# One raster for two operand pools, four changes of order, and later scales in a hybrid decoder trunk on one core

## The chip, the cores and the metric

The kernel runs on one core of one Trainium2 chip. The metric is the device time of one execution in microseconds (us). Engines: PE (TensorE; its weight loads are listed as PEld), DVE (VectorE), ACT (ScalarE), POOL (GpSimd), and SP (SyncE), which issues almost all DMAs in program order.

## The reference, cut to what matters

The kernel computes a two-layer trunk for 1,024 tokens and 1,024 channels in fp32.

```python
h = x
for layer in range(2):
    hn = rmsnorm(h, g_mix[layer])
    # layer 0: [b | c | x | u | v] = hn @ w_in ; gated conv (b, c, x) and spatial gating (u, v)
    # layer 1: latent attention (8 heads, causal) and a chunked matrix memory (4 heads)
    h = h + concat(branch_a, branch_b) @ w_out
    h = h + (silu(n @ w_gate) * (n @ w_up)) @ w_down          # n = rmsnorm(h, g_ffn), inner width 2816
    h = h + sigmoid(rmsnorm(h, g_ple) @ w_ple_gate) * (p[layer] @ w_ple_proj)
```

## The kernel before

**Split products.** Each fp32 operand is split into a high part (a cast to float32r, on ACT) and a low part (the remainder, on DVE): `split`, lines 146 and 147. A product of two split operands is three matmuls, in `mm3`: high x high at L189, high x low at L190, low x high at L191 (names in the trace end in h and l, or begin with them). Almost all of PE's work is such matmuls with 512 columns. The weights come in as fp32 tiles with the tag `raw` and are split into tiles `whi` and `wlo`.

**Memory.** Each pool is a range of SBUF addresses, the same in every partition. Pools lie one behind the other in the order in which they are opened: `const`, `opB` (operand slots 0 to 31, and others), `w` (`raw`, `whi`, `wlo`), `tmp` (temporaries, some of a few bytes), and behind them `opA` (slots 32 and up, `B.cp`), which is closed and opened again between stages, with the attention's pools in the same place. Operand tiles are 2,048 bytes per partition in all of them. From the sizes of the tiles: `opB` and `whi`/`wlo` tiles start at 832 modulo 2,048, and `opA` tiles at 1,984, since the small tiles of `tmp` lie between.

**Which operand lies where.** Both token halves of a matrix (n = 0 and 1) go through most products. In `opA` lie: all of x0 (the transposed input, `x_group`), 24 of the 40 slot numbers that `xc` takes (`free` at L452: 32 to 53, 54, 55; 16 to 31 are in `opB`), the half n = 1 of xp, and wj and pT of the output gates. In `opB` or `w` lie: xb, mix, act, xn, the half n = 0 of xp, and all other weights.

**Stages** (us of the profiled execution): input projection zv with token-major output 15 to 73; spatial gating (pu, pm) 73 to 132; conv branches (pc, px, pb) 132 to 266; output projection (po); FFN up and gate products (p) ; FFN down (pd) 690 to 988; gates and embedding (ppg, ppj) to 1,085; layer 1's projections to 1,378; attention with the memory interleaved to 1,600; the same tail again, with pd to 2,325 and `ple_out` from there to the end.

**Order.** A scheduler moves instructions within each engine, but the order in the code decides most. `later(d, fn)` calls fn after d more groups of matmuls (`tick`). `x_scale` makes the token scales of one half of the input: eight squares on ACT (L904, names junk and xt), then a reciprocal root, then `bcast_prep`, which puts the high and low parts of the scales on two diagonals dg, one on DVE and one on POOL; `bcast` multiplies both by ones on PE (Rb, L298 and L299), and ACT copies the sum to R. `norm_later` does the same elsewhere. In the gating, ug = pu * R on DVE (L1037) frees the PSUM bank of pu, then pm follows. `v_done` is the chain behind each tile of zv: gv on ACT, its square gvs on POOL, a reduction, a root, a product and a split on DVE. At the last keys, `heads_out` transposes k on PE (kTt), splits it on ACT and DVE, and stores it to kT_d; `load_head` reads K and Q of a head back (two tiles of 96 x 1,024 each). `mq_part(g, n)` is 24 matmuls for the memory's queries. `ple_out` transposes p (`make_pT`: ptr on PE, then a split into pTh and pTl), and per tile of 128 tokens multiplies gates (ppg) and embedding (ppj).

Of the kernel before, what the change touches and what calls it, by code (L numbers as in the profile page):

```python
# [11 lines left out]
F32 = mybir.dt.float32  # L12
# [9 lines left out]
P = 128  # L22
# [24 lines left out]
class Build:  # L47
# [60 lines left out]
    def w_part(self, srcs, kt, cols, name, gcol, slots=None):  # L108
        nc = self.nc
        raw = self.wp.tile([P, kt, cols], F32, tag="raw", name=self.name(f"r{name}"), bufs=RAW)  # L110
        o = 0
# [43 lines left out]
    def w_quarter(self, w, rows, c, name):  # L155

        t = self.wp.tile([P, 4, P], F32, tag="raw", name=self.name(f"r{name}"), bufs=RAW)
        self.nc.sync.dma_start(
            t, w[rows * HT : (rows + 1) * HT, c].rearrange("(k p) c -> p k c", p=P)
        )  # L160
        return t
# [7 lines left out]
    def w_chain(self, w, c0, c1, name, eng):  # L169


        tt = eng.tensor_tensor
        raw = lambda: self.wp.tile([P, 4, P], F32, tag="raw", name=self.name(f"s{name}"), bufs=RAW)
        a11 = self.w_quarter(w, 0, c0, name)
        a21 = self.w_quarter(w, 0, c1, name)
        a22 = self.w_quarter(w, 1, c1, name)
        a12 = self.w_quarter(w, 1, c0, name)
        s1, s2 = raw(), raw()
        tt(out=s1, in0=a21, in1=a22, op=ALU.add)
        tt(out=s2, in0=s1, in1=a11, op=ALU.subtract)  # L180
        tt(out=a21, in0=a11, in1=a21, op=ALU.subtract)
        return {1: a11, 2: a12, 4: a22, 5: s1, 6: s2, 7: a21}
# [95 lines left out]
    def bcast_prep(self, r):  # L278
# [6 lines left out]
        out = []  # L285
        for i, x in enumerate((rh.bitcast(F32), rl)):
            d = self.tmp("dg", (P, 4, P), F32R)
            (nc.vector, nc.gpsimd)[i].tensor_tensor(
                out=d, in0=self.ident.unsqueeze(1).to_broadcast([P, 4, P]),
                in1=x.unsqueeze(2).to_broadcast([P, 4, P]), op=ALU.mult,  # L290
            )
            out.append(d.rearrange("p a b -> p (a b)"))
# [32 lines left out]
def trunk(ctx, tc, x, p, positions, g_mix, g_ffn, g_ple, ev_w_in, ev_w_conv, ev_g_v, ev_w_s,  # L325
# [10 lines left out]
    B.wp = ctx.enter_context(tc.tile_pool(name="w", bufs=1))  # L336
    B.tp = ctx.enter_context(tc.tile_pool(name="tmp", bufs=1))

# [318 lines left out]
    def ffn_down(l, act_d, h_d, h2_d, X2, st, normed):  # L657
# [7 lines left out]
        def part(fh, ch, f, t=None):  # L665
            if t is None:
                t = B.wp.tile([P, HT], F32, tag="raw", name=B.name("rd"), bufs=RAW)
            r = (fh * half + f) * P
# [165 lines left out]
    def ple_out(l, tok, h2_d, X, r):  # L834

        pT = {}
        for n in range(2):
            pT[n] = make_pT(load_p(l, n) if n else tok, [32 + 4 * n + i for i in range(4)])
        for cg in range(2):
# [8 lines left out]
            for k in range(2):  # L848
                raw = B.wp.tile([P, HT], F32, tag="raw", name=B.name("rpj"), bufs=RAW)
                nc.sync.dma_start(raw, w_ple_proj[l][k * P : (k + 1) * P, c])  # L850
                a = B.slots2(40 + 4 * cg + 2 * k, 41 + 4 * cg + 2 * k, "wj")
                B.split(a[0], a[1], raw)
                wj.append(a)
            for tt in range(NT):
                n, t = tt // 4, slice((tt % 4) * P, (tt % 4 + 1) * P)
                pg = B.tm_mm(grp, X, tt, "ppg")
                pj = B.ps("ppj")
# [41 lines left out]
    def x_scale(n):  # L899
# [16 lines left out]

        B.later(2, fn)

    pv = B.ps_tr("pvec", (P, 16))
    nc.tensor.transpose(pv, rows0, ident[0:16, 0:16])  # L920
    nc.vector.tensor_copy(vec[:, 0:16], pv)
    for q in range(2):
        for kk in range(4):
            x_group(0, q, kk)
    zv_unit = B.w_unit(w_in[0:512, 2048:2560], 4, HT, "zva", G_MIX)
# [58 lines left out]
    for tt in range(NT):  # L984
        ps = B.tm_mm((zv_unit, HT), X, tt, "zv")
        if tt == 1:
# [3 lines left out]
        if tt < 4:  # L990
            for kk in range(2):
                x_group(1, tt // 2, (tt % 2) * 2 + kk)
            if tt == 3:
                x_scale(1)
        elif tt < 6:
            ws_T(tt - 4)
        elif tt == 6:
            u0 = u_unit(0, ((28, 29), (30, 31)))
# [84 lines left out]
    def rest(l, XC, second_half, h_d, out, rtok=None, full=True):  # L1083
# [4 lines left out]
        X2, st = newX(), {}  # L1088
        normed = lambda n: B.norm_later(st, n, 2 - n, out, rtok, full)
        prepare, run = ffn_down(l, act_d, h_d, h2_d, X2, st, normed)  # L1090
# [151 lines left out]
    def up_weights(src, kt, cols, gcol, name):  # L1242
        pairs = []
        half = cols // 2
        for k in range(kt):
# [3 lines left out]
            for i in range(2):  # L1249
                c = slice(i * half, (i + 1) * half)  # L1250
                raw = B.wp.tile([P, half], F32, tag="raw", name=B.name(f"r{name}"), bufs=RAW)
                nc.sync.dma_start(raw, src[k * P : (k + 1) * P, c])
# [282 lines left out]
    for n in range(2):  # L1535
        t = mq_part(0, n, B.ps("mq"))
        if kprev:
            heads_out(*kprev.pop(), ksc, kT_d, "kT")
# [15 lines left out]
    def load_head(h):  # L1554
        t = []
        for nm, src in (("K", kT_d), ("Q", qT_d)):
            for i in range(2):
                a = tp.tile([QK, T], F32R, tag=f"{nm}{i}", name=B.name(f"{nm}{i}"), bufs=2)
                nc.sync.dma_start(a.bitcast(F32), src[i][:, h, :].bitcast(F32))
                t.append(a)  # L1560
        return t

# [287 lines left out]
    for i, u in enumerate(units):  # L1850
# [5 lines left out]
        if i == 0:  # L1856
            mq_part(1, 0, psum("O", "mq", 1))
            att_scores(u)
            att_exp(u)
            ahead = 1  # L1860
            mq_part(1, 1, psum("m", "mq", 1))
            mem = mem_all()
# [82 lines left out]
```

## Time and profile before

| | us |
|---|---|
| median of 3 runs (lowest to highest) | 2453.76 (2452.49 to 2454.29) |
| profiled execution: its time | 2453.51 |
| profiled execution: span in the trace | 2451.8 |
| outside the span | 1.7 |
| PE busy | 2413.6 |
| DVE, ACT, POOL busy | 1561.2, 988.2, 679.8 |
| mean granted clock of PE | 0.999 |

Busy time of a matmul runs from its start to its modelled end; neighbours overlap, so that a 512-column matmul shows 389 ns where the next one starts some 227 ns behind it. PE is busy for nearly the whole span: a gain has to shorten matmuls or close the gaps that are left.

### The profile page before, as it was taken

To read this page: it belongs to the slowest core of one execution; us is meant where nothing else is said; L and a number is where in the kernel's file an instruction comes from. 1 tells how busy PE (TensorE), PEld (TensorE's weight loads), DVE (VectorE), ACT (ScalarE), POOL (GpSimd) and SP (SyncE) were. 2 spreads that over 40 slices of the span, in tenths; PEclk is the share of its full clock that TensorE was granted. 3 is DMA by queue.
4 is the path that set the end of the run, shared out by engine and by line. 5 is a ranking of instruction groups with operands and counts; after the bars stand their busy time and mean duration, and the time that the engine had idled before them with its cause. 6 is when DMAs were issued, how large, how long until landed. Compare 5 with 4: busy or idle time off the path is not lost.

```text
span 2451.8 us, 33875 instructions
## 1 busy us (share of the span) xinstructions
PE 2413.6 (98%) x11510; PEld 1993.8 (81%) x11510; DVE 1561.2 (64%) x3079; ACT 988.2 (40%) x1877; POOL 679.8 (28%) x678
## 2 busy tenths in 40 slices
PE   7999999999999999999999999999999999999999
PEld 6878887788888888888888788878788888888877
DVE  6864479645556778776785566548855455687731
ACT  5322244233233545444554455635333232454520
POOL 3452121546553000112321132111256556100000
PEclk9999999999999999999999999999999999999999
DMA  4221453433236966553454843154433233886721
GB/s 151 78 86 48 136 169 101 141 99 112 91 108 204 308 226 214 174 173 96 114 154 121 228 112 106 46 168 134 129 120 112 87 111 103 286 281 210 251 97 39
DMA packets 358685, 350.74 MB, mean 143 GB/s; under 512 B 24011, under 2 KB 249648, under 8 KB 358512
## 3 DMA queue, kind: packets, MB, share of 16 engines
q1 hardware_dynamic: 358016, 348.25, 45.3%
q8 instruction: 90, 1.47, 0.2%
q0 software_dynamic: 464, 0.33, 0.1%
q14 instruction: 83, 0.68, 0.1%
q10 hardware_dynamic: 32, 0.01, 0.0%
HBM read 255.18 MB, written 93.32 MB: 142 GB/s over the span
## 4 chain that ended last, share of the span: by engine, by line
PE 52%; DVE 4%; issue 2%; DMA 1%; ACT 1%; POOL 0%; SPq 0%; DVEq 0%; POOLq 0%; ACTq 0%
PE p L190 5%; PE p L189 5%; PE p L191 5%; PE pd L189 3%; PE pd L190 3%; PE pd L191 3%; PE O L1833 2%; PE ppg L191 2%; PE ppg L190 2%; PE ppg L189 2%; PE PT L1875 1%; PE po L189 1%; PE po L190 1%; PE po L191 1%; PE S L1775 1%
## 5 line engine op out<-in xcount | busy, mean ns | idle before, releaser
L189 PE MATMUL pd<-acth,hd 128*128 128x512 f32 x616 | 240.0, 390 | 0.1
L190 PE MATMUL pd<-actl,hd 128*128 128x512 f32 x616 | 239.7, 389 | 0.0
L191 PE MATMUL pd<-acth,ld 128*128 128x512 f32 x616 | 239.7, 389 | 0.0
L189 PE MATMUL p<-xch,hg 128*128 128x512 f32 x440 | 173.1, 394 | 5.3 <-DVE sg L534 2.2
L190 PE MATMUL p<-xcl,hg 128*128 128x512 f32 x440 | 173.1, 393 | 0.2
L189 PE MATMUL p<-xch,hu 128*128 128x512 f32 x440 | 173.0, 393 | 0.0
L191 PE MATMUL p<-xch,lu 128*128 128x512 f32 x440 | 172.9, 393 | 0.0
L191 PE MATMUL p<-xch,lg 128*128 128x512 f32 x440 | 172.9, 393 | 0.0
L190 PE MATMUL p<-xcl,hu 128*128 128x512 f32 x440 | 172.6, 392 | 0.0
L541 POOL TENSOR_TENSOR act<-act,sg 128x512 f32<-128x512 f32 x60 | 90.0, 1499 | 244.1 <-DVE act L534 239.3
L146 ACT CAST hu<-ru 128x512 fp32r<-128x512 f32 x116 | 71.6, 622 | 183.3 <-PE p L190 170.4
L189 PEld LDWEIGHTS pd<-acth,hd 128*128 128x128 f32 x616 | 115.6, 188 | 24.3 <-DVE res L728 0.5
L191 PEld LDWEIGHTS pd<-acth,ld 128*128 128x128 f32 x616 | 115.6, 188 | 24.3
L146 ACT CAST hg<-rg 128x512 fp32r<-128x512 f32 x110 | 68.2, 620 | 165.9 <-PE p L190 135.6
L190 PEld LDWEIGHTS pd<-actl,hd 128*128 128x128 f32 x616 | 115.6, 188 | 23.8
L147 DVE TENSOR_TENSOR lu<-ru,hu 128x512 fp32r<-128x512 f32 x116 | 117.2, 1011 | 14.9 <-ACT hu L146 14.9
L146 ACT CAST hd<-rd 128x512 fp32r<-128x512 f32 x110 | 68.3, 621 | 133.5 <-PE pd L190 82.2
L147 DVE TENSOR_TENSOR actl<-ra,acth 128x512 fp32r<-128x512 f32 x154 | 109.5, 712 | 12.1 <-ACT acth L146 12.0
L259 POOL TENSOR_TENSOR S<-S,sq 128x512 f32<-128x512 f32 x38 | 51.6, 1359 | 219.7 <-ACT sq L257 219.7
L147 DVE TENSOR_TENSOR ld<-rd,hd 128x512 fp32r<-128x512 f32 x110 | 76.9, 699 | 47.6 <-ACT hd L146 47.6
L189 PEld LDWEIGHTS p<-xch,hg 128*128 128x128 f32 x440 | 82.6, 188 | 26.5 <-ACT hg L146 3.0
L146 ACT CAST acth<-ra 128x512 fp32r<-128x512 f32 x154 | 94.7, 616 | 13.1 <-DMA ra<-act 9.3
(561 smaller groups left out, 6615.9 us busy)
## 6 DMA issues: line engine op xcount, KB each, us to landing
ra<-act SPq DMA_DIRECT2D x154, 256.0 KB, 3.7
rd<-in_w_down SPq DMA_DIRECT2D x154, 256.0 KB, 4.0
rg<-in_w_gate SPq DMA_DIRECT2D x100, 256.0 KB, 3.3
ru<-in_w_up SPq DMA_DIRECT2D x100, 256.0 KB, 2.9
act<-act SPq DMA_DIRECT2D x88, 256.0 KB, 2.0
act<-at SPq DMA_DIRECT2D x66, 256.0 KB, 2.0
rpg<-in_w_ple_gate SPq DMA_DIRECT2D x48, 256.0 KB, 3.0
sd<-in_w_down SPq DMA_DIRECT2D x44, 256.0 KB, 4.2
```

The source lines that it names most:

```text
L146: self.nc.scalar.copy(hi, src)
L147: (eng or self.nc.vector).tensor_tensor(out=lo, in0=src, in1=hi.bitcast(F32), op=ALU.subtract)
L189: mm(ps, a[0], b[0], start=first, stop=False, skip_group_check=more)
L190: mm(ps, a[0], b[1], start=False, stop=False, skip_group_check=more)
L191: mm(ps, a[1], b[0], start=False, stop=last, skip_group_check=more)
L259: eng.tensor_tensor(out=st[n], in0=st[n], in1=sq, op=ALU.add)
L541: (nc.vector if last else nc.gpsimd).tensor_tensor(out=t, in0=t, in1=sg[d["i"], key], op=ALU.mult)
L1775: mm(s[:, 0:w], q0, K0[:, c0 : c0 + w], start=True, stop=False)
L1833: nc.tensor.matmul(O[h][:, b * DV : (b + 1) * DV], t[:, j * P : (j + 1) * P], V[h // 2][:, kb, (h % 2) * DV : (h % 2 + 1) * DV], start=kb ...
L1875: nc.tensor.transpose(pt[:, j * P : (j + 1) * P], e[:, j * P : (j + 1) * P], ident)
```

## The change

Five edits. (1) `raw` moves to a pool of its own, and it and `tmp` go to the right end of SBUF (side="right"), so that `opA` and the attention's pools come right behind `w`. Worked out from the tile sizes, `opA` tiles then start at 832 modulo 2,048, as `opB` and `whi`/`wlo` do; `raw` goes from 832 to 2,016 and `tmp` from 832 to 864. (2) At the start, the first tile of zv runs its k-tiles 0 to 3 before the transposes for 4 to 7; the second half's transposes come four behind tile 1 and four behind tile 2 instead of two behind each of 0 to 3; `ws_T` and `u0` come one tile later, Rb two groups later. (3) In `bcast_prep` both diagonals are made on DVE. (4) The scales at the end of FFN down come at 2 + 2n groups instead of 2 - n. (5) The last `heads_out` follows `mq_part(0, 1)` instead of `mq_part(0, 0)`; head 0 is loaded in pieces; both `mq_part(1, n)` come before the first scores; and in `ple_out` the gate products of a tile are issued one tile ahead of its embedding product.

```diff
@@ w_part, and the same in four other places
-        raw = self.wp.tile([P, kt, cols], F32, tag="raw", name=self.name(f"r{name}"), bufs=RAW)
+        raw = self.rp.tile([P, kt, cols], F32, tag="raw", name=self.name(f"r{name}"), bufs=RAW)
@@ bcast_prep
-        for i, x in enumerate((rh.bitcast(F32), rl)):
+        for x in (rh.bitcast(F32), rl):
             d = self.tmp("dg", (P, 4, P), F32R)
-            (nc.vector, nc.gpsimd)[i].tensor_tensor(
+            nc.vector.tensor_tensor(
@@ trunk
     B.wp = ctx.enter_context(tc.tile_pool(name="w", bufs=1))
-    B.tp = ctx.enter_context(tc.tile_pool(name="tmp", bufs=1))
+    B.rp = ctx.enter_context(tc.tile_pool(name="raw", bufs=1, side="right"))
+    B.tp = ctx.enter_context(tc.tile_pool(name="tmp", bufs=1, side="right"))
@@ ple_out
-        for n in range(2):
-            pT[n] = make_pT(load_p(l, n) if n else tok, [32 + 4 * n + i for i in range(4)])
+        p_slots = lambda n: [32 + 4 * n + i for i in range(4)]
...
+            pgs = [B.tm_mm(grp, X, 0, "ppg")]
+            if cg == 0:
+                pT[0] = make_pT(tok, p_slots(0))
+                tok = load_p(l, 1)
             for tt in range(NT):
                 n, t = tt // 4, slice((tt % 4) * P, (tt % 4 + 1) * P)
-                pg = B.tm_mm(grp, X, tt, "ppg")
+                if tt + 1 < NT:
+                    pgs.append(B.tm_mm(grp, X, tt + 1, "ppg"))
+                if cg == 0 and tt == 1:
+                    pT[1] = make_pT(tok, p_slots(1))
+                pg = pgs[tt]
@@ x_scale
-        B.later(2, fn)
+        B.later(4, fn)
@@ input projection
-    for q in range(2):
-        for kk in range(4):
-            x_group(0, q, kk)
+    for kk in range(4):
+        x_group(0, 0, kk)
...
-        ps = B.tm_mm((zv_unit, HT), X, tt, "zv")
+        if tt == 0:
+            ps = B.ps("zv")
+            for k in range(KT):
+                if k == 4:
+                    for kk in range(4):
+                        x_group(0, 1, kk)
+                a = X[0][k]
+                B.mm3(ps, (a[0][:, 0:P], a[1][:, 0:P]), zv_unit[k], k == 0, k == KT - 1)
+            B.tick()
+        else:
+            ps = B.tm_mm((zv_unit, HT), X, tt, "zv")
...
-            for kk in range(2):
-                x_group(1, tt // 2, (tt % 2) * 2 + kk)
+            if tt in (1, 2):
+                for kk in range(4):
+                    x_group(1, tt - 1, kk)
@@ rest
-        normed = lambda n: B.norm_later(st, n, 2 - n, out, rtok, full)
+        normed = lambda n: B.norm_later(st, n, 2 + 2 * n, out, rtok, full)
@@ last keys
         t = mq_part(0, n, B.ps("mq"))
-        if kprev:
+        if n == 1:
             heads_out(*kprev.pop(), ksc, kT_d, "kT")
@@ load_head
+        if h == 0:
+            last, rest = slice(T - P, T), slice(0, T - P)
+            for nm, i, c in (("Q", 0, last), ("K", 0, slice(0, T)), ("Q", 1, last),
+                             ("K", 1, slice(0, T)), ("Q", 0, rest), ("Q", 1, rest)):
+                part(nm, i, c)
@@ attention, first unit
-            mq_part(1, 0, psum("O", "mq", 1))
+            for n in range(2):
+                mq_part(1, n, psum(("O", "m")[n], "mq", 1))
             att_scores(u)
             att_exp(u)
             ahead = 1
-            mq_part(1, 1, psum("m", "mq", 1))
```

Three places in the order of issue. First, ACT in the input projection, before the change, around the last two casts of the second half's x0 (x0h_571 and x0h_580); the junk rows are the last two of eight squares over the second half, vh belongs to `v_done`:

```order
L904 ACTIVATE junk_597,ss_584<-xt_264 128x512
L904 ACTIVATE junk_599,ss_584<-xt_266 128x512
L146 CAST vh_151_537<-gv_146_516 128x512
L146 CAST x0h_571<-xT_566 128x512
L146 CAST x0h_580<-xT_575 128x512
L934 ACTIVATE gv_177_626<-zv_541,rt_287 128x512
```

The same place with the change; the last two casts are x0h_519 and x0h_528, and junk_588 is the first of the eight squares:

```order
L146 CAST x0h_501<-xT_496 128x512
L146 CAST x0h_510<-xT_505 128x512
L146 CAST vh_135_467<-gv_130_446 128x512
L146 CAST x0h_519<-xT_514 128x512
L146 CAST x0h_528<-xT_523 128x512
L912 ACTIVATE junk_588,ss_587<-xt_219 128x512
```

The eight squares stood ahead of the last two casts and now stand behind them. Second, PE at the first scores, before (S is a tile of scores, mq_13298 is `mq_part(1, 1)`; 12 of its matmuls stand behind the first score, and the last here is the first of them):

```order
L190 MATMUL mq_13298<-xnl_2361_9896,hmq_0_2953_13086 128x512
L191 MATMUL mq_13298<-xnh_2360_9895,lmq_0_2954_13087 128x512
L1775 MATMUL S_13279<-K_2967_13182,Q_2969_13186 128x512
L1776 MATMUL S_13279<-K_2968_13184,Q_2969_13186 128x512
L1775 MATMUL S_13283<-K_2967_13182,Q_2969_13186 128x512
L1776 MATMUL S_13283<-K_2968_13184,Q_2969_13186 128x512
L189 MATMUL mq_13298<-xnh_2376_9960,hmq_4_2956_13092 128x512
```

The same place with the change (mq_13284 is `mq_part(1, 1)`; S_13348 belongs to the second unit of scores):

```order
L190 MATMUL mq_13284<-xnl_2413_10107,hmq_4_2956_13095 128x512
L191 MATMUL mq_13284<-xnh_2412_10106,lmq_4_2957_13096 128x512
L1807 MATMUL S_13313<-K_2968_13187,Q_2967_13185 128x512
L1808 MATMUL S_13313<-K_2970_13191,Q_2967_13185 128x512
...
L1809 MATMUL S_13317<-K_2968_13187,Q_2969_13189 128x512
L1811 LDWEIGHTS identb
L1811 MATMUL S_13317<-maskq,identb 128x128
L1807 MATMUL S_13348<-K_2968_13187,Q_2967_13185 128x512
```

All of mq now stands ahead of the first score, and no mq between the first unit of scores and the second. Third, PE in `ple_out` of layer 1, before, where the first ppj stands; ppg_22835 is the first tile of gates:

```order
L189 MATMUL ppg_22835<-hpg_7_5443_22803,xph_22543 128x512
L189 MATMUL ppj_22880<-wjh_22825,pTh_22724 128x512
L190 MATMUL ppj_22880<-wjl_22826,pTh_22724 128x512
L189 MATMUL ppg_22897<-hpg_0_5422_22761,xph_22116 128x512
L190 MATMUL ppg_22897<-lpg_0_5423_22762,xph_22116 128x512
L792 MATMUL ptr_22741<-ident,ptok_22737 128x128 x2
L191 MATMUL ppj_22880<-wjh_22825,pTl_22725 128x512
```

With the change, where the transposes ptr and the first ppj stand; ppg_22800 and ppg_22847 are the first and the second tile of gates:

```order
L191 MATMUL ppg_22800<-hpg_7_5429_22768,xpl_22549 128x512
L793 MATMUL ptr_22825<-ident,ptok_22642 128x128 x2
...
L189 MATMUL ppg_22847<-hpg_0_5408_22726,xph_22121 128x512
...
L191 MATMUL ppg_22847<-hpg_7_5429_22768,xpl_22549 128x512
L189 MATMUL ppj_22872<-wjh_22790,pTh_22830 128x512
L190 MATMUL ppj_22872<-wjl_22791,pTh_22830 128x512
```

A whole tile of gates (24 matmuls) now stands between the transposes and the first ppj, and the transposes for the second half no longer stand in the middle of the first ppj.

## Rows read from the trace of the kernel before

**Rows 1.** Page, part 1: busy time, share of the span, instructions.

```profile
PE 2413.6 (98%) x11510; PEld 1993.8 (81%) x11510; DVE 1561.2 (64%) x3079; ACT 988.2 (40%) x1877; POOL 679.8 (28%) x678
```

**Rows 2.** Groups of PE by form: line, tile, count; busy, mean ns; idle before.

```profile
L190 PE MATMUL pd<-actl,hd 128*128 128x512 f32 x616 | 239.7, 389 | 0.0
...
L190 PE MATMUL p<-xcl,hg 128*128 128x512 f32 x440 | 173.1, 393 | 0.2
...
L191 PE MATMUL p<-xbh,lg 128*128 128x512 f32 x176 | 68.6, 390 | 0.0
...
L190 PE MATMUL pc<-x0l,hc 128*128 128x512 f32 x64 | 25.3, 395 | 0.0
```

**Rows 3.** Tile ppg on PE, 985 to 1030 us: ns min/median/max, starts.

```profile
L190 PE MATMUL ppg<-xpl,hpg x33: 389/389/395, 1000.1 to 1029.8; 128*128 128x512 f32 x33
```

**Rows 4.** The same, 1040 to 1085 us.

```profile
L190 PE MATMUL ppg<-xpl,hpg x50: 389/392/404, 1040.1 to 1084.6; 128*128 128x512 f32 x50
```

**Rows 5.** Windows, PE alone: window, length, PE busy, clock, DMA share, GB/s.

```profile
800.00:920.00 120.00, 120.00 (x531) 1.00 0.80 265
```

**Rows 6.** Waits of PE over the span: us in total, times, longest.

```profile
PE zv L189 <- ACT x0h L146: 4.0, 1, 4.0
...
PE S L1775 <- DMA Q<-qTd: 1.7, 1, 1.7
PE pm L189 <- DVE ug L1037: 1.7, 1, 1.7
...
PE kTt L1290 <- DVE k L1503: 1.5, 1, 1.5
...
PE ptr L792 <- DVE lpg L147: 1.0, 1, 1.0
...
PE ppj L189 <- ACT pTh L146: 0.7, 1, 0.7
```

**Rows 7.** Timeline of ACT: start us, us, instruction.

```profile
46.25 0.64 ACT L904 ACTIVATE junk<-xt 128x512 f32<-128x512 f32 x1
...
51.67 1.06 ACT L146 CAST x0h<-xT 128x512 fp32r<-128x512 f32 x2
```

**Rows 8.** Windows: length; busy of PE, PEld, DVE, ACT, POOL; clock; DMA.

```profile
48.00:56.00 8.00, 3.99 (x14) 2.65 (x13) 7.22 (x25) 5.36 (x17) 0.89 (x1) 0.79 0.14 38
...
70.00:90.00 20.00, 20.00 (x88) 16.11 (x87) 18.81 (x42) 6.79 (x12) 10.14 (x10) 1.00 0.38 107
90.00:110.00 20.00, 20.00 (x105) 16.94 (x104) 17.25 (x32) 6.07 (x11) 8.25 (x6) 1.00 0.19 63
...
126.00:134.00 8.00, 5.73 (x40) 5.04 (x39) 7.15 (x11) 2.29 (x4) 2.45 (x4) 1.00 0.41 131
```

**Rows 9.** Timeline of DVE, with the idle time before.

```profile
61.28 0.69 DVE L941 TENSOR_REDUCE v<-gvs 128x8 f32<-128x512 f32 x1 [2.33 <-POOL z L1047]
```

**Rows 10.** Line 288, the diagonals: ns min/median/max, and who waited.

```profile
L288 DVE TENSOR_TENSOR dg<-ident,rh x10: 679/684/686, 27.9 to 1688.7; 128x512 fp32r<-128x512 f32 x10
L288 POOL TENSOR_TENSOR dg<-ident,rl x10: 1279/1367/1422, 28.2 to 1688.8; 128x512 fp32r<-128x512 f32 x10
...
  PEld Rb L299: 3.8, 6
  PE Rb L299: 1.5, 4
```

**Rows 11.** Timeline of SP (queue times) at the last keys.

```profile
1367.13 0.58 SPq L1296 DMA_DIRECT2D kTd<-kTl  x1
...
1371.71 1.00 SPq L1559 DMA_DIRECT2D K<-kTd  x2
```

**Rows 12.** Tile K, 1360 to 1400 us: its DMA.

```profile
DMA to landing us min/median/max: 3.5/5.5/10.5
```

**Rows 13.** Timeline of PE at the first scores and at the first PT.

```profile
1377.50 0.39 PE L191 MATMUL mq<-xnh,lmq 128*128 128x512 f32 x1
1379.56 0.47 PE L1775 MATMUL S<-K,Q 96*128 96x512 f32 x1 [1.68 <-DMA Q<-qTd]
...
1381.73 0.23 PE L1779 MATMUL S<-maskq,identb 128*128 128x128 bf16 x1
...
1386.39 0.61 PE L1875 MATMUL PT<-ident,P 128*128 128x128 f32 x4
```

More of the change, by code (lines that the diff above doesn't have):

```diff
@@ L155, in w_quarter @@
     def w_quarter(self, w, rows, c, name):
-        t = self.wp.tile([P, 4, P], F32, tag="raw", name=self.name(f"r{name}"), bufs=RAW)
+        t = self.rp.tile([P, 4, P], F32, tag="raw", name=self.name(f"r{name}"), bufs=RAW)
         self.nc.sync.dma_start(
@@ L172, in w_chain @@
         tt = eng.tensor_tensor
-        raw = lambda: self.wp.tile([P, 4, P], F32, tag="raw", name=self.name(f"s{name}"), bufs=RAW)
+        raw = lambda: self.rp.tile([P, 4, P], F32, tag="raw", name=self.name(f"s{name}"), bufs=RAW)
         a11 = self.w_quarter(w, 0, c0, name)
@@ L666, in part @@
             if t is None:
-                t = B.wp.tile([P, HT], F32, tag="raw", name=B.name("rd"), bufs=RAW)
+                t = B.rp.tile([P, HT], F32, tag="raw", name=B.name("rd"), bufs=RAW)
             r = (fh * half + f) * P
@@ L848, in ple_out @@
             for k in range(2):
-                raw = B.wp.tile([P, HT], F32, tag="raw", name=B.name("rpj"), bufs=RAW)
+                raw = B.rp.tile([P, HT], F32, tag="raw", name=B.name("rpj"), bufs=RAW)
                 nc.sync.dma_start(raw, w_ple_proj[l][k * P : (k + 1) * P, c])
@@ L990, in trunk @@
         if tt < 4:
-            for kk in range(2):
-                x_group(1, tt // 2, (tt % 2) * 2 + kk)
+            if tt in (1, 2):
+                for kk in range(4):
+                    x_group(1, tt - 1, kk)
             if tt == 3:
                 x_scale(1)
-        elif tt < 6:
-            ws_T(tt - 4)
-        elif tt == 6:
+        elif tt < 7:
+            if tt > 4:
+                ws_T(tt - 5)
+        else:
             u0 = u_unit(0, ((28, 29), (30, 31)))
@@ L1250, in up_weights @@
                 c = slice(i * half, (i + 1) * half)
-                raw = B.wp.tile([P, half], F32, tag="raw", name=B.name(f"r{name}"), bufs=RAW)
+                raw = B.rp.tile([P, half], F32, tag="raw", name=B.name(f"r{name}"), bufs=RAW)
                 nc.sync.dma_start(raw, src[k * P : (k + 1) * P, c])
@@ L1554, in load_head, with part @@
     def load_head(h):
-        t = []
-        for nm, src in (("K", kT_d), ("Q", qT_d)):
-            for i in range(2):
-                a = tp.tile([QK, T], F32R, tag=f"{nm}{i}", name=B.name(f"{nm}{i}"), bufs=2)
-                nc.sync.dma_start(a.bitcast(F32), src[i][:, h, :].bitcast(F32))
-                t.append(a)
-        return t
+        t = {}
+        def part(nm, i, c):
+            src = (kT_d if nm == "K" else qT_d)[i]
+            a = t.get((nm, i))
+            if a is None:
+                a = tp.tile([QK, T], F32R, tag=f"{nm}{i}", name=B.name(f"{nm}{i}"), bufs=2)
+                t[nm, i] = a
+            nc.sync.dma_start(a[:, c].bitcast(F32), src[:, h, c].bitcast(F32))
+        if h == 0:
[3 more added lines that the diff above has]
+                part(nm, i, c)
+        else:
+            for nm in "KQ":
+                for i in range(2):
+                    part(nm, i, slice(0, T))
+        return [t["K", 0], t["K", 1], t["Q", 0], t["Q", 1]]
     heads = {0: load_head(0)}
```

## The prediction

> **What bounds the kernel now.** I read the page first: PE is busy for 98% of the span, and no other engine for more than 64% [rows 1]. So I asked two things: is each matmul as short as it could be, and what fills the 38 us in which PE idles.
>
> For the first I took the groups of PE's instructions with different forms kept apart. All large products are the same instruction, 128x512 from the same kinds of tile, and still their mean durations differ: 389 ns in pd, 390 in p on xb, 393 in p on xc, 395 in the conv products on x0 [rows 2]. The reader is to see that the order follows where the operand lies: pd and xb have both operands in opB and w, x0 has one wholly in opA, and xc has 24 of its 40 slots there. If a matmul with one operand in opA costs 6 ns more (395 less 389), xc should show 389 + 0.6 x 6 = 392.6, and it shows 393. The cleanest pair is ppg in the middle of the kernel: same line, same weights, same stage, only the token half differs. The first half (opB) has a median of 389 ns, the second (opA) 392 [rows 3, 4]. What distinguishes opA from opB and w is its start modulo 2,048 bytes.
>
> For the second I listed PE's waits [rows 6]. Those that the change touches are zv on the casts of x0 (4.0 us), S on the load of Q (1.7), pm on ug (1.7), kTt on k (1.5), and ptr and ppj in the output gates (1.0 and 0.7). The waits inside FFN up and in the attention proper are not touched.
>
> **The layout.** Matmuls after the gating stage with an operand in opA: 1,584 of p (60% of the 2,640 on xc), 576 of conv, half of ppg's 768, and 96 of ppj. At 6 ns the first two give 9.5 and 3.5 us; ppg at the 3 ns of its own rows gives 1.2, and ppj 0.3 to 0.6. That is 14.6; the mean of p also holds matmuls behind a wait, so I take **-14 us**. Bounds: 0 if the raster is not the cause, and -16 if ppg and ppj too cost 6 ns. The 144 matmuls of pu and the 192 of zv also have x0 in opA (336 x 6 ns = 2 us), but I don't count them here: that stage is DVE's, as the next part shows. Nothing else has to give way for this term: PE is busy throughout those stages, and DVE and SP wait for it. The other half of the layout edit, raw and tmp at new offsets, I cost at nothing. DVE, ACT and DMA have room: in the pd stage, the densest in loads, DMA is busy 80% of the time [rows 5].
>
> **The start.** PE waits 4.0 us for the last two casts of x0, and then runs at a granted clock of 0.79 in that window, where it is busy for 3.99 us [rows 6, 8]. The casts are late because ACT took up eight squares at 46.25 us and reached the casts only at 51.67 [rows 7]. With the change the casts go first. On PE that is worth the wait, 4.0 us, and (1 - 0.79) x 3.99 = 0.8 us of clock, and the layout adds 2 us before the gating: PE alone would be 6.8 us earlier. But from 70 us on DVE is busy 94%, 86%, and at the end 89% of the time, with PE's next wait, pm on ug, right there [rows 6, 8]: what PE gains it waits for again unless DVE too is earlier. DVE gains for certain only one hole: its reduction at 61.28 us had waited 2.33 us. The row names POOL's z, but POOL takes gvs in program order behind its diagonal, which waits for DVE's rl, and that diagonal goes away [rows 9]. The price is two diagonals more on DVE, 2 x 0.68 = 1.4 us [rows 10]. So the bounds are -0.9 (2.33 - 1.4, DVE otherwise as full as now) and -6.8 (PE's gain passes whole). DVE's work behind the first tiles of zv also starts earlier, by how much no row says; the busy shares speak for the near end, and I take **-3 us**.
>
> [...]
>
> **Both diagonals on DVE.** The second Rb waited for POOL's diagonal at all ten places: 3.8 us at the weight load and 1.5 at the matmul, 5.3 in all, 0.53 each. The diagonal takes 1.37 us on POOL, 0.68 on DVE [rows 10]. Both start with DVE's rl or just behind it, and DVE's second comes behind its first, so it ends at 1.37 instead of 1.37 plus POOL's start: about 0.2 to 0.3 us sooner, and where Rb's two groups are apart the wait vanishes. Two of the ten lie in the input projection (counted above) and move two groups later; one more, the second half's at the end of FFN down, moves three groups later and loses its wait of 0.5. I take 0.2 to 0.25 at each of seven other places and that 0.5: **-2 us**. Bounds: 0 (DVE busy with something else at that moment) and -4 (all waits gone). The later scales cost nothing as long as the gates' first half covers them: three groups are 3 x 24 x 0.227 = 16 us, and the first half's gates run for some 30 us before the second half's [rows 3, 4]. Without that cover it would be one wait of PE as long as the delay.
>
> **Last keys and first scores.** Now PE waits 1.5 us for k and 1.7 for Q. With kTt behind 24 more matmuls (5.5 us) k is ready. But the stores of kT then come 5.5 - 1.5 = 4.0 us later, the last at 1371.1 instead of 1367.1 [rows 11]. Before, K's load was issued 4.6 us behind that store, with a store of mq between; that puts it at 1374.5 to 1375.7, and it lands 3.5 to 5.5 us on, at 1378 to 1381 [rows 11, 12]. PE, without its waits and with the 12 remaining matmuls of mq ahead (2.7 us), gets to the first score at 1377.7 - 1.5 + 2.7 = 1378.9 [rows 13]. So up to 2 us of stall is left, I take 0.5, and 2.7 of 3.2 are gained. Against it: between the last of the first unit's scores and the first PT (1381.73 to 1386.39, 4.66 us) PE had 23 matmuls, of which nine were mq, 2.0 us [rows 13]. DVE's maximum and ACT's exponentials set that distance. The change leaves 17 matmuls there (three for the memory's decay come up from behind PT), so some 1.2 us of it turns into idle time. Net **-1.5 us**; bounds -3.2 (the new idle time is covered) and +1 (K lands last and the cover is gone).
>
> **Output gates.** ptr's 1.0 and ppj's 0.7 us of waiting go [rows 6]: 24 matmuls (5.5 us) now stand between the transposes and the first ppj, and the lpg that ptr waited for in line is no longer needed there. Nothing is added. **-1.7 us**, bounds 0 and -2.5.
>
> **Sum.** -14 - 3 - 2 - 1.5 - 1.7 = -22.2. The profiled execution took 2453.5 us, 0.25 under the median of the runs, so 2453.5 - 22.2 = 2431.3, and I say **2431**. A measurement of this kernel can tell about 0.2%, 5 us.
>
> **The rivals.** *The raster is not the cause.* The second halves in opA could be slower for what else runs beside them (conv, FFN up), or by distance. Then only the order edits count: 2453.5 - 8.2 = **2445**. For it: nothing ties 6 ns to an address but four groups and a pair. Against it: the pair of ppg, and 392.6 against 393. [...] Chance 0.15.
>
> *The start is not capped.* If DVE's busy share is padded by its own waiting inside instructions, PE's 6.8 us pass whole, 3.8 more than I count: **2427.5**. For it: DVE was idle 2.33 us in the middle of its crowded stretch [rows 9]. Against: 94% [rows 8]. Chance 0.12.
>
> *The moves of order give back what they take.* The keys cost +1, the start gives -0.9, dg and gates half: 2453.5 - 14 - 0.9 + 1 - 1 - 0.9 = **2437.7**. Chance 0.13.
>
> *Slower, by the loads.* raw tiles were at 832 and go to 2,016 modulo 2,048, off the raster that their neighbours keep. If writes to such tiles are longer, pd feels it first: one 256 KB tile each 12 matmuls (2.7 us), and DMA 80% busy [rows 5]. Up to 25% longer it is hidden. Beyond that each per cent costs one per cent of the two pd stages (1,848 matmuls x 0.227 = 420 us), 4.2 us. To eat 22 us and 5 more takes 6.5 per cent beyond, thus packets a third longer: **2459** or more. Against it: nothing in the trace shows loads to depend on the address. Chance 0.05.
>
> **How the numbers follow.** My forecast has 0.55, and 2427 to 2436 as its own range. The 80% range leaves out the slower rival and part of the first: **2422 to 2446**, where 2422 is the uncapped start with the full bounds of layout, dg and gates (-16, -6.8, -4, -1.5, -2.5 make -30.8). Faster than 2448.9: all cases but the slower one and a small part of the first, 0.87; within 0.2%: 0.07; slower: 0.06.
>
> **What would show it.** After the change, pc, px, pb and p on xc should stand at 389 to 390 ns, with pd unchanged; ppg's halves should be equal. If conv stays at 395, the raster is not the cause, and the time is near 2445. The wait of zv on x0h should be gone and that of pm on ug grown, to 3 us or more; if pm waits no longer than now, the start was not capped. Rb on dg should show under 3 us over ten. S on K's load should stay under 1 us, and a wait of PT on ACT's P, about 1 us, should be new. In the gates neither ptr nor ppj should wait. I would be wrong if the slow matmuls' cause is the stage, or if a new wait in front of the first PT or in FFN up takes more than these terms give.

## The result and the profile after

The changed kernel takes 2434.46 us (median of 4 runs, 2430.95 to 2437.73) against 2453.69 beside it: ratio 0.9922, 95% interval 0.9905 to 0.9939, thus 15 to 23 us less, and 19 in the middle. That is faster by more than the 5 us that can be told; 2431 was forecast. The profiled execution took 2430.95 us, 22.6 less than the profiled one of before, where the sum said 22.2.

PE's groups by form, of the changed kernel, in the columns of [rows 2]:

```profile
L190 PE MATMUL pd<-actl,hd 128*128 128x512 f32 x616 | 239.7, 389 | 0.0
L190 PE MATMUL p<-xcl,hg 128*128 128x512 f32 x440 | 172.3, 392 | 0.2
...
L191 PE MATMUL p<-xbh,lg 128*128 128x512 f32 x176 | 68.6, 389 | 0.0
...
L190 PE MATMUL pc<-x0l,hc 128*128 128x512 f32 x64 | 24.9, 389 | 0.0
```

Conv has gone from 395 to 389 ns and pd has not moved [rows 2]. p on xc shows only one ns less in this line; its hu products show 389 to 390, and the hg products carry the waits and slow clock of FFN up, to which I come. The second half's ppg, at 392 before [rows 4], now stands with the first:

```profile
L190 PE MATMUL ppg<-xpl,hpg x48: 387/389/395, 1030.6 to 1071.7; 128*128 128x512 f32 x48
```

PE's waits in the changed kernel, to be held against [rows 6]:

```profile
PE p L189 <- DVE u L595: 4.1, 2, 2.1
PE pm L189 <- DVE ug L1056: 3.7, 3, 3.0
...
PE zv L189 <- ACT hzva L150: 2.8, 1, 2.8
PE mq L189 <- DVE kTl L151: 1.8, 1, 1.8
...
PE S L1807 <- ACT P L1830: 1.4, 1, 1.4
PE Rb L298 <- DVE ws L147: 1.3, 1, 1.3
...
PE p L189 <- ACT p L582: 1.3, 2, 0.6
```

Gone are zv on x0h (4.0), S on Q, kTt on k, ptr and ppj. In their place stand pm on ug, grown from 1.7 to 3.7, and four that were not there: zv on its first weights, mq on kTl, S on P, and Rb on a split of ws that DVE now takes ahead of it. FFN up's wait for u at L595 has grown from 1.7 us to 4.1. Its wait for sg, 2.2 us before, is gone, so that all waits of p together grew from 6.1 us to 7.7.

Where the time came from is seen in the lengths of stretches, each from the first start of one tile on PE to that of the next, read from the four traces (us; layout alone and order alone are the first two experiments):

| stretch | before | after | layout alone | order alone |
|---|---|---|---|---|
| start to pc | 132.25 | 129.17 | 131.80 | 129.52 |
| pc to po (conv) | 133.92 | 130.66 | 132.25 | 133.93 |
| p to pd (FFN up, layer 0) | 432.10 | 427.63 | 426.73 | 432.10 |
| pd to ppg | 212.73 | 212.03 | 212.71 | 212.06 |
| ppg to the next projection | 115.29 | 112.71 | 113.64 | 114.42 |
| first kTt to the first yaT (keys, first part of attention) | 147.46 | 148.24 | 150.47 | 148.34 |
| p to pd (FFN up, layer 1) | 431.92 | 426.90 | 427.03 | 431.68 |
| first ppg of layer 1 to the end | 126.50 | 123.68 | 124.54 | 124.67 |

A stretch of two kernels that are alike in it differs by up to 1 us between executions: FFN up of layer 0 takes 432.10 us before and 432.98 in the kernel with the later scales alone (below). And the granted clock was lower for a while in some entries: in the changed kernel 0.93 from 415 to 440 us, behind a wait for u in FFN up of layer 0, which is worth 1.7 us (0.07 of 25); with the layout alone 0.89 from 130 to 145 us, in conv, and 0.89 from 1350 to 1365 us, at the keys.

### The profile page after: what moved, and what is told of

It reads as the page before. It is cut to its first block, busy times and chain, and to the rows that moved or that the text cites. A ratio compares the mean times of both kernels' runs of the same rounds, so it can differ in the third digit from the quotient of the medians.

```text
span 2429.2 us, 33861 instructions
## 1 busy us (share of the span) xinstructions
PE 2393.5 (99%) x11502; PEld 1995.3 (82%) x11510; DVE 1559.9 (64%) x3089; ACT 986.8 (41%) x1877; POOL 671.8 (28%) x668
## 4 chain that ended last, share of the span: by engine, by line
PE 86%; DVE 8%; DMA 2%; issue 2%; ACT 1%; POOL 0%; SPq 0%; DVEq 0%; ACTq 0%; POOLq 0%
PE p L190 10%; PE p L189 10%; PE p L191 10%; PE pd L189 5%; PE pd L191 5%; PE pd L190 5%; PE po L189 2%; PE ppg L189 2%; PE ppg L191 2%; PE po L191 2%; PE ppg L190 2%; PE po L190 2%; PE O L1865 2%; PE PT L1907 1%; PE lat L189 1%
## 5 line engine op out<-in xcount | busy, mean ns | idle before, releaser
L189 PE MATMUL pd<-acth,hd 128*128 128x512 f32 x616 | 240.0, 390 | 0.3 <-DVE res L729 0.3
L191 PE MATMUL pd<-acth,ld 128*128 128x512 f32 x616 | 239.7, 389 | 0.0
L190 PE MATMUL pd<-actl,hd 128*128 128x512 f32 x616 | 239.7, 389 | 0.0
L189 PE MATMUL p<-xch,hg 128*128 128x512 f32 x440 | 172.1, 392 | 5.7 <-DVE u L595 4.1
L190 PE MATMUL p<-xcl,hg 128*128 128x512 f32 x440 | 172.3, 392 | 0.2
L189 PE MATMUL p<-xch,hu 128*128 128x512 f32 x440 | 171.5, 390 | 0.8 <-DVE act L535 0.8
L191 PE MATMUL p<-xch,lg 128*128 128x512 f32 x440 | 172.0, 391 | 0.0
L190 PE MATMUL p<-xcl,hu 128*128 128x512 f32 x440 | 171.3, 389 | 0.0
L191 PE MATMUL p<-xch,lu 128*128 128x512 f32 x440 | 171.2, 389 | 0.0
L189 PEld LDWEIGHTS pd<-acth,hd 128*128 128x128 f32 x616 | 115.6, 188 | 24.4 <-DVE res L729 0.7
L191 PEld LDWEIGHTS pd<-acth,ld 128*128 128x128 f32 x616 | 115.6, 188 | 24.1
L190 PEld LDWEIGHTS pd<-actl,hd 128*128 128x128 f32 x616 | 115.6, 188 | 24.0
L189 PEld LDWEIGHTS p<-xch,hg 128*128 128x128 f32 x440 | 83.0, 189 | 25.2 <-issue 5.4
```

Source lines behind the costliest of these rows:

```text
L189: mm(ps, a[0], b[0], start=first, stop=False, skip_group_check=more)
L190: mm(ps, a[0], b[1], start=False, stop=False, skip_group_check=more)
L191: mm(ps, a[1], b[0], start=False, stop=last, skip_group_check=more)
```

## The experiments

**Layout and order apart.** First the layout alone on the kernel before:

```diff
-    B.tp = ctx.enter_context(tc.tile_pool(name="tmp", bufs=1))
+    B.rp = ctx.enter_context(tc.tile_pool(name="raw", bufs=1, side="right"))
+    B.tp = ctx.enter_context(tc.tile_pool(name="tmp", bufs=1, side="right"))
```

> The kernel before with nothing changed but the layout (raw in a pool of its own, raw and tmp at the right end). Raster theory: conv (pc, px, pb) at 389 ns instead of 395, p on xc at 390 instead of 393, the halves of ppg equal; with no change of order the time falls by 12 to 16 us, to about 2440 us, and FFN up waits somewhat more for DVE than before. Rival, the stage and not the address makes the matmuls slow: conv stays at 395 and the time within 2 us of 2453.7, so that the 19 us of the whole change would have to come from the order.

Measured: 0.9941 of the kernel before (0.9929 to 0.9954), 14.5 us less; px and pb at 389 ns, pc at 398 to 402 in the stretch of lower clock. Then the reverse, all of the order on the old layout:

> The changed kernel with the layout of before (raw and tmp between w and opA). Raster theory: conv stays at 395 ns, p on xc at 393, and the order edits alone give 5 to 9 us (start -3, diagonals -2, gates -2 to -3, keys 0), thus 2445 to 2449 us. Rival, the order gives nothing by itself because DVE and the new waits take it back: 2452 to 2454 us. If the two halves do not interfere, this gain and that of the layout alone add up to the 19 us of the whole change.

Measured: 0.9974 (0.9964 to 0.9985), 6.4 us less; conv stays at 395. One line of each, layout alone first:

```profile
L190 PE MATMUL pb<-x0l,hb 128*128 128x512 f32 x64 | 24.9, 389 | 0.0
```

```profile
L190 PE MATMUL pb<-x0l,hb 128*128 128x512 f32 x64 | 25.3, 395 | 0.0
```

The two add up to 20.9 us, the whole change gives 19.2: within the intervals no interference can be told. The rival that the stage makes the matmuls slow is out, since the same stage with the same order changes by 6 ns with the layout alone; the next two runs shift x0 against the weights and leave the stage's order alone.

**How the raster works.** The changed kernel with gaps between the tiles of x0:

```diff
-        t = B.slots2(i, i + 1, "x0")
+        t = B.slots2(i, i + 1, "x" + "abcdefghijklmnop"[8 * n + k])
+        if i < 62:
+            nc.gpsimd.memset(B.cp.tile([P, 8], F32, tag=f"gap{i}", name=f"gap{i}"), 0.0)
```

> The changed kernel with a gap of 32 bytes behind each pair of x0 tiles, so that the 16 pairs (names xa to xp: token half 0 with k 0 to 7, then half 1) start at 0, 32, 64, ... 480 bytes beyond the raster of w (320 modulo 2048 here, since 512 bytes of constants are saved). Raster theory with a period of 256 bytes: in conv the pairs xa and xi stand at 389 ns, others up to 395, and the second eight repeat the first eight. With a period of 512 only xa is short; with a period of 64 every second one is short; a period of 32 or none makes all equal. Rival, no effect of the address: all 16 equal, at 389 or at 395.

Measured: in px the second eight repeat the first eight to 1 ns (on xal and xil 392 and 392, on xdl and xll 396 and 397, on xfh and xnh 400 and 400 in L191), so the period in this run is 256 bytes. But no pair is at 389 in all three lines, xa and xi (equal starts) not either: a pair's time is not its own affair. Conv takes 133.98 us there, against 130.66 in the changed kernel. So I made the rasters uniform over each token half:

```diff
-        t = B.slots2(i, i + 1, "x0")
+        if i in (32, 48):
+            w = 16 if n == 0 else 48
+            nc.gpsimd.memset(B.cp.tile([P, w], F32, tag=f"gap{i}", name=f"gap{i}"), 0.0)
+        t = B.slots2(i, i + 1, "xq" if n else "xr")
```

> The changed kernel with uniform rasters: the eight pairs of x0 of token half 0 (names xrh, xrl) start 64 bytes beyond the raster of w, those of half 1 (xqh, xql) 256 bytes beyond it. Theory after the run with 16 rasters (period of 256 bytes, and the cost falls on neighbours too, so that mixed rasters cost everywhere): half 1 stands at 389 ns in conv as if nothing were moved, half 0 at 392 to 397. Rival, only an equal start modulo 2,048 is short: both halves are above 392. Rival, 64 bytes are enough: both at 389.

Measured over all of conv, half 0 stands at 393 to 394, 389 to 390 and 392 to 393 ns in the three lines, lower than I expected in the second, and half 1 (256 bytes) seemed to fail with 392 to 393, 389 to 390 and 391. Conv takes 132.05 us. Single groups of 24 matmuls tell why. Tile pb in that kernel, first a stretch of half 0, then the start of the group on half 1, then its end (columns as in [rows 3]):

```profile
L189 PE MATMUL pb<-xrh,hb x5: 394/394/394, 153.5 to 156.2; 128*128 128x512 f32 x5
L190 PE MATMUL pb<-xrl,hb x5: 388/388/388, 153.7 to 156.5; 128*128 128x512 f32 x5
L191 PE MATMUL pb<-xrh,lb x5: 392/392/392, 154.0 to 156.7; 128*128 128x512 f32 x5
```

```profile
L189 PE MATMUL pb<-xqh,hb x4: 389/395/398, 157.6 to 159.7; 128*128 128x512 f32 x4
```

```profile
L189 PE MATMUL pb<-xqh,hb x3: 389/389/389, 160.4 to 161.7; 128*128 128x512 f32 x3
```

The group on half 1 begins at 156.9 us. It is slow (up to 398 ns) for some ten matmuls behind the half with the other raster, and then exactly at 389. So 256 bytes were as good as none once it had settled; 64 bytes cost 2 ns on the mean of three lines (394, 388 and 392 against 389), 128 (the kernel before, at 395) 6. The change of raster between neighbours cost these ten slow matmuls besides.

In conv the weights kept their start modulo 256 in every run, so these runs leave a rival: that the operand whose 512 columns are streamed (the moving operand) has a good place of its own, whatever the weights do. The trace of the kernel before answers it. In the gates of layer 1 the streamed operand is hpg or lpg, which stays in `w`, and the one loaded is xp. The median is 389 ns while xp lies in `opB` (first line) and 393 once it lies in `opA` (second). And ppj, with both operands in `opA`, stands at 389 between the gates of the first half (third; 391 and 389 in L189 and L191):

```profile
L190 PE MATMUL ppg<-lpg,xph x16: 387/389/395, 2344.5 to 2356.5; 128*128 128x512 f32 x16
```

```profile
L190 PE MATMUL ppg<-lpg,xph x32: 390/393/404, 2359.0 to 2386.1; 128*128 128x512 f32 x32
```

```profile
L190 PE MATMUL ppj<-wjl,pTh x6: 389/389/389, 2342.7 to 2357.9; 128*128 128x512 f32 x6
```

So it is the two starts against each other that count in these rows. Between the slow gates of the second half (2359 to 2386 us) ppj too is slow (a median of 394 ns in this line and 396 in L191), as the pairs xa and xi were between neighbours of another raster (397, 392 and 394 in px).

**The start and the diagonals.** The second diagonal back on GpSimd, and, apart from it, the order of before in the input projection:

```diff
-        for x in (rh.bitcast(F32), rl):
+        for i, x in enumerate((rh.bitcast(F32), rl)):
             d = self.tmp("dg", (P, 4, P), F32R)
-            nc.vector.tensor_tensor(
+            (nc.vector, nc.gpsimd)[i].tensor_tensor(
```

> The changed kernel with the second diagonal back on GpSimd. Theory: the second Rb waits for POOL again, 0.25 to 0.7 us at the four to six places behind the gating stage, together 1.5 to 2.5 us; in the input projection DVE has 1.4 us less to do but waits for POOL's gvs behind the diagonal, so conv begins at 129 to 131 us (129.2 in the changed kernel). Rival, the diagonal on DVE costs as much as it saves: conv begins before 128.5 us and the whole time does not change by more than 1 us.

> The changed kernel with the order of before in the input projection and Rb two groups later as before, diagonals on DVE and the new layout kept. Theory: the wait of zv for the casts of x0 is back at about 4 us and that of pm for ug falls from 3.7 to 1.5 to 2 us, since DVE sets the end of this stage: of the 4 us and the slow clock behind them only 2 to 3 us are lost, conv begins at 131 to 132 us. Rival, the start is not capped by DVE: conv begins at 134 to 136 us and pm waits as long as in the changed kernel.

Conv begins at 129.17 us in the changed kernel, at 130.01 with the diagonal on GpSimd, at 129.53 with the old order, and at 131.80 with both as before (layout alone). So each of the two edits by itself gives most of the 2.6 us, and the second adds only 0.4 or 0.8 (four later kernels with the start of the changed one begin conv at 129.01 to 129.40, so 0.4 is hardly clear of scatter). They do not do it in the same way. With the diagonals on DVE and the old order, DVE's wait for POOL's gvs is gone. In the changed kernel it is still there, 2.93 us where it was 2.33 [rows 9], because POOL takes two products on ru, whose load it had waited for, ahead of gvs (ACT had the gv for it at 50.4 and 53.6 us):

```profile
57.62 0.69 DVE L948 TENSOR_REDUCE v<-gvs 128x8 f32<-128x512 f32 x1 [2.93 <-POOL gvs L946]
```

```profile
54.27 2.32 POOL L118 TENSOR_TENSOR ru<-ru,vec 128x512 f32<-128x512 f32 x2 [14.58 <-DMA ru<-in_ev_w_in]
```

The new order also brings DVE's work forward. From 28 to 48 us DVE is busy 16.82 us in the kernel before and 18.25 in the changed one with the diagonal on GpSimd, that is by the order and not by the diagonals (columns of [rows 8]; that these 1.4 us are what conv gains is likely and not shown):

```profile
28.00:48.00 20.00, 20.00 (x101) 16.40 (x99) 16.82 (x39) 8.63 (x18) 10.42 (x10) 1.00 0.30 82
```

```profile
28.00:48.00 20.00, 20.00 (x104) 16.97 (x103) 18.25 (x50) 11.27 (x27) 8.99 (x9) 1.00 0.29 79
```

My theory for the old order was thus wrong in size (131 to 132 expected). That DVE sets the end of this stage holds: with the old order PE waits 2.5 us for x0h, but pm then only 1.2 for ug, instead of none and 3.7. Windows of that run, in the columns of [rows 8], show DVE as full as ever:

```profile
48.00:56.00 8.00, 5.21 (x17) 3.69 (x16) 7.12 (x24) 4.44 (x12) 1.04 (x1) 0.79 0.26 66
70.00:90.00 20.00, 20.00 (x96) 16.81 (x95) 19.33 (x44) 6.20 (x11) 10.82 (x10) 1.00 0.39 107
```

At Rb behind the gating stage the diagonal on GpSimd costs 0.32, 0.32, 0.67 and 0.29 us in the stretches of four places, 1.6 in all. In a fifth, FFN down of layer 1, the changed kernel is the longer one (210.90 us against 210.34), but kernels alike there lie anywhere from 210.34 to 211.09. With it, line 299 waits again (weight loads and matmuls):

```profile
  POOL dg L288: 4.3, 8
```

**The later scales.** The kernel before with nothing but this:

```diff
-        normed = lambda n: B.norm_later(st, n, 2 - n, out, rtok, full)
+        normed = lambda n: B.norm_later(st, n, 2 + 2 * n, out, rtok, full)
```

> The kernel before with nothing changed but the delay of the scales at the end of FFN down (2 + 2n groups instead of 2 - n). Theory: the second Rb of the second half loses its wait of some 0.5 us and the first Rb its wait for the gates, so the stretch from the first gates of layer 0 to the projections of layer 1 is 0.5 to 0.9 us shorter, and nothing else moves. Rival, a reader of the later scales waits: that stretch is longer.

Measured: 114.46 instead of 115.29 us from the first ppg to the next projection, 0.8 less; with the whole order it is 114.42. The stretches behind it differ from the kernel before by -0.8 to +1.0 us, FFN up ahead of it, which the edit cannot touch, by +0.9: a late reader does not show. The one execution took 2454.71 us, among the 2453.62 to 2459.44 of the kernel before beside it, which settles nothing. So the later scales are a gain of their own, and free as far as these stretches can tell.

**The last keys.** The transposes in the middle of `mq_part(0, 1)`:

```diff
+        for k in range(KT):
+            if mid and k == 4:
+                mid()
+            B.mm3(ps, mq_units[g][k], X[n][k], k == 0, k == KT - 1)
```

> The changed kernel with the last transposes of k in the middle of mq_part(0, 1), with 12 of its matmuls ahead and 12 behind. Theory: in the changed kernel the 1.8 us that PE waits for kTl comes from the switch of the PSUM pools right behind the transposes; with 12 matmuls (2.7 us) behind them it goes to under 0.3 us and k is still ready, so this place is 1.5 to 2 us shorter than in the changed kernel; the wait of S for P (1.4 us) stays. Rival, kTl is late for another reason, such as ACT or DVE being busy: the wait stays above 1 us. The whole time: 2429 to 2436 us, in which 2 us cannot be told.

Measured: the wait for kTl is gone, as it should be if what follows the transposes waits for the old PSUM pool to be read out (that the pools are the cause is argued from the code; the run shows that 12 matmuls behind the transposes cover it). But the stretch to the first yaT is 148.46 us, as in the changed kernel (148.24): PE now gets to the scores before the loads. In that run:

```profile
1365.52 0.50 PE L1812 MATMUL S<-K,Q 96*128 96x512 f32 x1 [0.80 <-DMA K<-kTd]
...
1368.41 0.50 PE L1813 MATMUL S<-K,Q 96*128 96x512 f32 x1 [0.75 <-DMA Q<-qTd]
...
1371.43 0.51 PE L1811 MATMUL S<-K,Q 96*128 96x512 f32 x1 [1.41 <-ACT P L1834]
```

**The output gates.** The order of before in `ple_out` on the changed kernel:

> The changed kernel with the output gates in the order of before. Theory: the waits of ptr and ppj come back, but smaller than before the change (1.7 us), since the layout alone already left only 0.8 us there; with the order of transposes ahead of the first gates the last stage is 1.5 to 2.5 us longer than in the changed kernel. Rival, the layout alone had removed them: less than 1 us.

Measured: the last stretch is 127.14 us instead of 123.68. Some 2.2 of these 3.5 us are one wait of ptr for the load of p, which then comes last on SP's queue, and behind it the granted clock is 0.94 from 2300 to 2330 us. The waits that the change aimed at have moved there.

**A version beyond both.** The largest wait left is p on u in FFN up. In the changed kernel DVE forms sums of weights ahead of u, and waits for a load to do so; PE then waits for u:

```profile
418.79 1.61 DVE L179 TENSOR_TENSOR sg<-rg,rg 128x512 f32<-128x512 f32 x1 [1.45 <-DMA rg<-in_w_gate]
```

```profile
422.83 0.47 PE L189 MATMUL p<-xch,hg 128*128 128x512 f32 x1 [1.97 <-DVE u L595]
```

GpSimd, which idled for 62.6 us up to 408.93, can form those of the third pair:

```diff
-                eng = nc.vector if d in ahead + third else nc.gpsimd
+                eng = nc.vector if d in ahead else nc.gpsimd
```

I ran it first together with the keys in the order of before, then with the keys as changed:

> The changed kernel with the last keys, head 0's loads and the first scores in the order of before, and in FFN up the sums for the third pair of weights on GpSimd instead of DVE. Theory: the keys' order costs about 1 us net (a wait for kTl and one for P in place of two), which comes back; the longest waits of FFN up for DVE (u at L595, 4.1 us, with 1.5 us of slow clock behind one of them) fall below 2 us because DVE has six to eight additions less ahead of u: 2427 to 2431 us, 3 to 6 us less than the changed kernel's median of 2434. Rival, POOL's sums take twice as long, and the weights they make are late: a new wait of p for a weight's cast, and no gain or a loss.

> The changed kernel with one edit more: in FFN up the sums for the third pair of weights on GpSimd instead of DVE; the keys stay as changed. Theory: the two waits of p for u (4.1 us) go in both layers, as in the run with the old keys, and the keys keep their time, since the order of before costs 3 us more under the new layout: 2423 to 2427 us, ratio to the kernel before about 0.986. Rival, the gain of that run came from the keys: the time stays at 2430 to 2434 us.

Measured: 0.9875 (0.9859 to 0.9892) and 0.9872 (0.9856 to 0.9889), 31 us less than the kernel before, 2426.38 and 2426.63 us. The changed kernel was not timed beside them; against its trace the second's FFN up falls to 424.15 and 423.65 us, 3.5 and 3.2 less. Some 1.7 of the 3.5 is clock, 0.93 in the changed kernel behind its wait for u and 1.00 in the last version:

```profile
415.00:440.00 25.00, 23.03 (x95) 0.93 0.60 188
```

```profile
415.00:440.00 25.00, 25.00 (x112) 1.00 0.59 189
```

Nobody waits at L595 any more; PE's waits in layer 0's FFN up are these:

```profile
PE p L189 <- DVE o L553: 0.7, 1, 0.7
PE p L189 <- ACT p L582: 0.7, 1, 0.7
PE p L189 <- DVE act L535: 0.6, 1, 0.6
```

The order of the keys makes no difference to the total between these two; that it costs 3 us under the new layout, as I had written, is not borne out.

## Why the prediction was right, and where not

**Layout, -14.** Right in mechanism and size: -14.5 timed alone, and by stretches of the whole change against the order alone -3.3 in conv, -4.5 and -4.8 in FFN up (9.5 forecast for p; layout alone against before, without a stretch of lower clock, -5.4 and -4.9), -1.7 and -1.0 at the gates. Equal halves of ppg, conv at 389, pd unmoved came as named. The 96 ppj were counted for an operand in `opA`, but both of theirs lie there, and they are slow only between slow gates (394 ns in L190 there, 389 before). The rival "stage, not raster" is refuted by the two runs apart. What I left out: "PE is busy throughout those stages, DVE and SP wait for it" was wrong for the beginning of FFN up. There shorter matmuls bring PE sooner to DVE's results: the wait for u grew from 1.7 to 4.1 us (4.0 with the layout alone), while that for sg went. The last version shows that what stood there was worth 6.7 us in the two layers, the clock behind it included.

**Start, -3.** Measured -2.6 beside the layout (129.17 against 131.80). The cap by DVE was right, and pm's wait grew to 3.7 us as forecast. But the hole in DVE's work from which the near bound was made did not close: DVE waits 2.93 us for gvs in the changed kernel. DVE's earlier work, which the prediction named and left without a price, is what the traces show in its place, so that 2.6 came so close to 3 is in part luck. The clock behind PE's wait (the window's 0.21 of 8 us is 1.7 us, where the prediction took 0.8) did not come back either. It is 1.00 from 48 to 56 us now, and lower behind pm's wait of 3.0 us, where it was 1.00 before [rows 8]:

```profile
90.00:110.00 20.00, 16.69 (x79) 13.76 (x78) 16.51 (x31) 6.03 (x10) 9.56 (x8) 0.91 0.23 79
```

Of the edits, the diagonal moved off POOL gives 2.3 us alone, the order alone 1.8, and the two overlap.

**Diagonals and later scales, -2.** Measured -1.6 at four Rb and -0.8 for the later scales, -2.4 in all. One Rb gained a new wait behind a split of ws on DVE, 1.3 us for PE, inside the start's term.

**Last keys, -1.5.** The term that failed: nothing was gained. The stretch is 0.8 us longer than before, inside the bounds (-3.2 to +1) but on the other side of nothing. Even the 0.8 is not clear of scatter: the kernel with the later scales alone has the keys of before and takes 148.45 us from the first kTt to the first yaT, because its two waits are longer than those of [rows 6]:

```profile
PE S L1775 <- DMA Q<-qTd: 2.4, 1, 2.4
PE kTt L1290 <- DVE k L1503: 1.8, 1, 1.8
```

Both old waits went, and 0.5 us of stall on K was not needed. In their place came S on P, 1.4 us, which I had priced at 1.2, and mq on kTl, 1.8 us, which I had not seen: I let `mq_part(1, 0)` follow the transposes as free cover, and it could not begin before DVE had split them. In the changed kernel, PE between the transposes and mq:

```profile
1352.41 1.03 PE L1309 MATMUL kTt<-ident,k 128*96 128x128 f32 x8
1355.27 0.50 PE L189 MATMUL mq<-xnh,hmq 128*128 128x512 f32 x1 [1.83 <-DVE kTl L151]
```

**Gates, -1.7.** Mis-sized: with the order alone the last stretch is 1.8 us shorter and the one ahead of it, at whose end the transposes stood, another 1.0, as long as ptr's wait; that is -2.8, just past the far bound of -2.5. On the new layout the same order gives only 0.9 and 0.2 (124.54 to 123.68, 211.13 to 210.90), since the layout alone had already taken 2.0 from the last stretch.

**The rival of slower loads.** A 256 KB tile of rd landed after 4.0 us before and lands after 4.2 now, of ra 3.7 and 3.8; PE's stretch of pd does not show it. The cover that I named holds.

**The sum.** -22.2 forecast, -22.6 between the profiled executions, -19.2 between the medians. What the trace of one execution cannot give is the scatter. In part the executions differ by stretches at a lower granted clock. In the stretch from 1410 to 1440 us, first in the changed kernel, then in the last version, whose code there is the same (it runs some 2.5 us earlier):

```profile
1410.00:1440.00 30.00, 28.76 (x211) 1.00 0.42 115
```

```profile
1410.00:1440.00 30.00, 28.89 (x187) 0.89 0.41 115
```

One such stretch costs about 3 us (0.11 of 30). That the 3.4 us between the profiled executions and the medians come from these is not shown, since only one execution of the changed kernel has a trace, and the clock is not the whole of it: the execution of 2435.15 us had a mean granted clock of 0.998, the profiled one of 2430.95 us 0.997.

## What to carry to other kernels

Read the same instruction form across stages before looking for gaps: 6 ns on 389 told more here than all waits together, and the operands' start addresses explained it. Where matmuls get shorter, ask which engine PE will now catch up with; the gain that came back last (6.7 us) lay in one line that chose DVE for sums while GpSimd idled. And when an instruction is moved ahead as cover, look at what it waits for itself: here mq stood still for 1.8 us, until DVE had split the last tile of the PSUM pool closed just before it (that the pool is the reason is argued from the code), and so was no cover.

## What the runs showed of the hardware that I had not expected

In these runs the mean of a 512-column matmul in float32r went with how far apart its two operands start modulo 256 bytes: 389 ns at equal starts (conv in the changed kernel), 391 at 64 bytes apart and again 389 at 256 (pb in the kernel with two rasters, once settled), 395 at 128 (conv before). It was not a price per matmul: it ran in a fixed pattern from one matmul to the next (394, 388, 392 at 64 bytes), and behind a change of raster some ten matmuls stayed longer (389 to 398 ns in L189) until the pattern settled, even where the new raster was the matching one.
